# A feature-major first stage in a one-core hybrid diffusion layer: x loaded transposed, norm factors as one row, one visit per step to the row products, two short first steps

## The chip, the cores and the metric

The kernel is one program on one core of a Trainium2 chip. The metric is the device time of one execution in microseconds (us). One execution was also taken by the hardware profiler; all durations below come from that one.

## The reference

One layer with model width D = 2048, 256 latent tokens `x` and 256 context tokens `ctx`. The part that matters here is its beginning: the modulation vectors, the normalised and modulated activations h, and the first of the projections of h.

```python
mod  = (silu(c)     @ w_mod + b_mod)[:, None, :]      # 2048 -> 6 * 2048
modc =  silu(c_ctx) @ w_mod + b_mod
sh1, sc1, g1, sh2, sc2, g2 = split(mod, 6)            # the same for modc
h  = rms_norm(x,   norm_w[0]) * (1 + sc1)  + sh1      # 256 x 2048
hc = rms_norm(ctx, norm_w[0]) * (1 + sc1c) + sh1c
q, ff, fb, v, g, a, b = split(h @ w_in)               # the same for hc; v is 1024 wide
... # recurrence and convolution, output projection, residual, conv FFN, residual
```

`rms_norm(x, w)` is `x * rsqrt(mean(x*x) + 1e-6) * w`. Everything is float32.

## The kernel before

**Number format.** Each float32 operand of a large product is cut into a high part (rounded to fp32r by ScalarE, `self.split`, L976) and a low rest (subtracted by VectorE, L977). One product then takes three matmuls: high by high, high by low, low by high (`mm3_x`, L206 to L208; `mm3_w`, L197 to L199).

**Stages.** The first stage, `phase0`, computes shift and scale for both token sets, h transposed (`hT`: features on the partitions, 16 blocks kb of 128 features, the 512 tokens of x and ctx along the free dimension), and the projection v of all 512 tokens. Then come the gemms of eight heads, with recurrence and convolution work beside them, the output projection, and the FFN up and down.

**The first stage before.** x and ctx arrive token-major in four blocks b of 128 tokens. For each block ScalarE (one of the squares: VectorE) sums the squares (`square_x`), VectorE and GpSimd make the factor (`factor_x`; the power -1/2 is GpSimd's, L229), VectorE scales the block (`scale_x`), and TensorE transposes it, 128 features by 128 tokens at a time (`first_x`, `transpose_x`). The stage runs in eight steps q of two feature blocks:

- `gemv_row(q, t)`, t = 0 to 3: loads 1 MB of `w_mod` and multiplies by silu(c) and silu(c_ctx), four narrow matmuls side by side (L470); after t = 3 ScalarE copies the sums out of PSUM (L475).
- `columns(q)`: four transposes turn these rows into columns (L481), then four small VectorE instructions (L483 to L492) leave scale A and shift B of the step's features.
- `make_h(q)`: ScalarE applies A and B to the transposed x (L510), and `split` writes both parts of `hT`.
- `v0(q, b)` and `v1(q, b)`: the left and right 512 columns of v for token block b. `v0` adds up in PSUM over all steps (`vps`, four banks). `v1` starts a new PSUM tile at each step, which VectorE adds to a running sum in SBUF (`v1_add`, L541). The weights for it (`v_raw`, two SBUF buffers) are split into `vw` by `v_load`.

The row products of step q stand in the program one step ahead of their use, in two visits (t = 0, 1 and t = 2, 3) with `v1` between them. Eight 1 MB buffers (tags raw, whi, wlo in turn) hold the `w_mod` tiles, so loads run two steps ahead. The orders of TensorE and of the DMA queue (SyncE, SP) are written out by hand in the whole stage, those of ScalarE and VectorE only to the end of the hand-written beginning (`self.order(P0_ENG | {ET.Activation, ET.DVE})`); after it a scheduler orders these two by priority. `step(q, b)` runs `transpose_x`, `columns` and `make_h` at high priority. PSUM of the stage: four banks for `vps`, one for the rows, three (tag ax) for everything else. `gemv(n)` starts pieces of the later modulation vectors, which are VectorE work (L713), and `wtile(0)` the first weights of the next stage.

Of the kernel before, what the change touches and what calls it, by code (L numbers as in the profile page):

```python
# [8 lines left out]
F32 = mybir.dt.float32  # L9
# [6 lines left out]
P = 128  # L16
D = 2048
# [12 lines left out]
P0_ROW = 1  # L30
P0_PRIO = 300
P0_X, P0_C = 0, 0
# [13 lines left out]
WIDE, NARROW = (0, 0), (16, 16)  # L46
LEVELS = (1, 2, 4, 8, 16, 32, 64)
# [66 lines left out]
class _Kernel:  # L114
# [126 lines left out]
    def run(self):  # L241
# [43 lines left out]
        p0x, px = enter(name="p0x", bufs=4 - P0_ROW, space=PSUM)  # L285
# [63 lines left out]
    def consts(self):  # L349
# [7 lines left out]
        self.mhalf = cst.tile([P, 2], F32, name="mhalf")  # L357
# [53 lines left out]
    def phase0(self, p0, px, srcs):  # L411
        nc, a = self.nc, self.a
        x0, big = self.x0, self.big
        rstd = p0.tile([P, 4], F32, name="rstd0")

        def load_x(b):
            src = a["x"] if b < 2 else a["ctx"]
            rows = src[0, (b % 2) * P:(b % 2 + 1) * P, :]
            nc.sync.dma_start(x0[:, b, :], rows[:, 0:512])
            nc.sync.dma_start(self.big0[:, b, :], rows[:, 512:1024])  # L420
            nc.sync.dma_start(big[:, :, b, :], rows[:, 1024:].rearrange("p (n c) -> p n c", n=2))

        sums = {}

        def square_x(b, i):

            if i == 0:
                sums[b] = self.sm.tile([P, 5], F32, tag="ss5", name="ss5", bufs=4)
            ss = sums[b][:, i:i + 1]
            src = (x0[:, b, :], self.big0[:, b, :], big[:, :, b, :])[i]  # L430
            if i == 0 and b:
                junk = p0.tile([P, 512], mybir.dt.bfloat16, tag="mkv", name="junkv")
                nc.vector.scalar_tensor_tensor(junk, src, 1.0 / D, src, op0=ALU.mult, op1=ALU.mult, accum_out=ss)
            else:
                junk = p0.tile([P, 2, 512], mybir.dt.bfloat16, tag="mk", name="junk")
                nc.scalar.activation(junk if i == 2 else junk[:, 0, :], src, AF.Square, scale=D ** -0.5, accum_out=ss)

        def factor_x(b):
            ss = sums[b]
            nc.vector.tensor_scalar(ss[:, 3:4], ss[:, 0:1], ss[:, 1:2], EPS, op0=ALU.add, op1=ALU.add)  # L440
            nc.vector.tensor_add(ss[:, 4:5], ss[:, 3:4], ss[:, 2:3])
            self.rsqrt(rstd[:, b:b + 1], ss[:, 4:5])

        def scale_x(b, i):
            x = (x0[:, b, :], self.big0[:, b, :], big[:, :, b, :])[i]
            nc.vector.tensor_scalar_mul(x, x, rstd[:, b:b + 1])

        self.nt = 0
        vps = [self.mm_tile("v") for _ in range(4)]
        vw = self.vx.tile([P, 2, 2, 1024], F32R, tag="vx", name="vw")  # L450
        rows = {}

        vt = p0.tile([P, 4, 256], F32, name="vt")

# [3 lines left out]
        for i in range(2):  # L458
            nc.vector.tensor_copy(cz[:, :, i], self.cs[:, i * KB:(i + 1) * KB])

        def gemv_row(q, t):

            if t == 0:
                rows[q] = px.tile([P, 512], F32, tag="row", name="row", bufs=P0_ROW)
            tag, n = (("raw", 3), ("whi", 3), ("wlo", 2), ("raw", 3), ("whi", 3), ("wlo", 2), ("raw", 3), ("whi", 3))[self.nt % 8]
            self.nt += 1
            w = self.stg.tile([P, 2048 if tag == "raw" else WBUF], F32, tag=tag, name="mraw", bufs=n)[:, 0:2048]
            nc.sync.dma_start(w, a["wm1"][q, t])
            for g in range(4):
                nc.tensor.matmul(rows[q][g * 32:(g + 1) * 32, :], cz[:, t * 4 + g, :], w[:, g * 512:(g + 1) * 512],  # L470
                                 start=t == 0, stop=t == 3)
            if t == 3:
                r = p0.tile([P, 512], F32, tag="rows", name="rows")
                with self.tc.high_priority(P0_PRIO):
                    nc.scalar.copy(r, rows[q])  # L475
                rows[q] = r

        def columns(q):
            col = self.ax_tile("col")
            for i in range(4):  # L480
                nc.tensor.transpose(col[:, i * P:(i + 1) * P], rows[q][:, i * P:(i + 1) * P], self.ident)  # L481
            cv = self.sm.tile([P, 2, 2, 2], F32, tag="cv", name="cv", bufs=2)
            nc.vector.reduce_sum(cv, col.rearrange("p (s j g c) -> p s j c g", s=2, j=2, g=4)[:, :, :, 0:2, :],  # L483
                                 axis=mybir.AxisListType.X)
            A = self.ab[:, 1, q * 2:(q + 1) * 2, :]
            B = self.ab[:, 0, q * 2:(q + 1) * 2, :]
            bsh = self.par("bmod", q * 2, 2).unsqueeze(2).to_broadcast([P, 2, 2])
            bsc = self.bsc1[:, q * 2:(q + 1) * 2].unsqueeze(2).to_broadcast([P, 2, 2])
            nw = self.par("nw", q * 2, 2).unsqueeze(2).to_broadcast([P, 2, 2])
            nc.vector.tensor_add(B, cv[:, 0], bsh)  # L490
            nc.vector.tensor_add(A, cv[:, 1], bsc)
            nc.vector.tensor_mul(A, A, nw)  # L492

# [785 lines left out]
```

## Time and profile before

| | us |
|---|---|
| runs shown (three) | 1422.15, 1422.55, 1440.83; median 1422.55 |
| profiled execution: its own time | 1419.87 |
| profiled execution: span | 1418.1 |
| TensorE busy in the span | 1375.5 (97%) |
| VectorE / ScalarE busy | 1073.3 (76%) / 716.6 (51%) |
| data read | 323.58 MB, 231 GB/s over the span |

The lines of the profile name an instruction by its line, its engine, its operation and its output and input tiles. Times in timelines count from the start of the span. Matmuls are pipelined: the shown duration of one overlaps the next, so the distance between starts is what one costs.

### The profile page before, as it was taken

Reading aid. Unit: us, or ns where it says so; the run is one execution under the profiler, and the core shown is the slowest. Engines: PE = TensorE matmul, PEld = TensorE weight load, DVE = VectorE, ACT = ScalarE, POOL = GpSimd, SP = SyncE. Lnnn points to the kernel's source line nnn. Section 1 sums busy time; section 2 is a strip of 40 time slices with the busy share of each in tenths; the row PEclk is TensorE's granted clock in tenths of the full one; section 3 lists DMA queues with packets and bytes.
Section 4 is the critical chain, followed back from the end, with each engine's and each line's share of the span. In section 5 each row is a group of like instructions: output and inputs, shape, how many; then the busy total and the mean of one; then the engine's idle time right before and its main releaser. Section 6 shows DMA issues by size and latency. Waiting matters only on the chain.

```text
span 1418.1 us, 24793 instructions
## 1 busy us (share of the span) xinstructions
PE 1375.5 (97%) x10272; PEld 1224.9 (86%) x10272; DVE 1073.3 (76%) x1577; ACT 716.6 (51%) x1174; POOL 31.2 (2%) x57
## 2 busy tenths in 40 slices
PE   4999999999999999999999999999999999999997
PEld 2566888888888898988999999999999998888886
DVE  4444788999999899777788788778878886767544
ACT  4333456666656665536744444454545443333532
POOL 0000001001000011000000000000000000000000
PEclk9999999999999999999999999999999999999999
DMA  9988676446645565788355555555555558878652
GB/s 374 391 325 330 258 267 218 160 188 238 222 167 207 208 226 189 286 305 302 123 205 180 205 185 203 181 206 189 199 184 203 193 194 340 312 287 306 242 187 106
DMA packets 49153, 329.38 MB, mean 232 GB/s; under 512 B 5392, under 2 KB 5648, under 8 KB 10896
## 3 DMA queue, kind: packets, MB, share of 16 engines
q1 hardware_dynamic: 49040, 327.80, 62.7%
q8 instruction: 80, 1.31, 0.4%
q14 instruction: 33, 0.27, 0.1%
HBM read 323.58 MB, written 4.19 MB: 231 GB/s over the span
## 4 chain that ended last, share of the span: by engine, by line
PE 77%; DVE 11%; ACT 4%; DMA 3%; issue 2%; POOL 2%; SPq 0%; DVEq 0%; POOLq 0%; ACTq 0%
PE val L197 6%; PE val L199 6%; PE val L198 6%; PE dn L206 6%; PE gate L197 6%; PE dn L208 6%; PE gate L199 5%; PE dn L207 5%; PE gate L198 5%; DVE wlo L140 3%; DVE acc L930 3%; PE v L206 2%; PE wo L208 2%; PE wo L206 2%; PE wo L207 2%
## 5 line engine op out<-in xcount | busy, mean ns | idle before, releaser
L137 ACT CAST whi<-raw 128x2048 fp32r<-128x2048 f32 x193 | 368.9, 1912 | 371.3 <-PE val L198 120.1
L140 DVE TENSOR_TENSOR wlo<-raw,whi 128x2048 fp32r<-128x2048 f32 x193 | 441.9, 2289 | 149.4 <-PE dn L207 59.7
L199 PE MATMUL val<-h,wlo 128*128 128x256 f32 x704 | 194.3, 276 | 0.0
L197 PE MATMUL val<-h,whi 128*128 128x256 f32 x704 | 194.3, 276 | 0.0
L198 PE MATMUL val<-h,whi 128*128 128x256 f32 x704 | 194.3, 276 | 0.0
L197 PE MATMUL gate<-h,whi 128*128 128x256 f32 x688 | 189.9, 276 | 0.0
L198 PE MATMUL gate<-h,whi 128*128 128x256 f32 x688 | 189.9, 276 | 0.0
L199 PE MATMUL gate<-h,wlo 128*128 128x256 f32 x688 | 189.9, 276 | 0.0
L1139 DVE SCALAR_TENSOR_TENSOR gacc<-gate,params,gacc 128x189 f32<-128x189 f32 (+2 forms) x352 | 152.4, 433 | 23.3 <-ACT gacc L1133 12.5
L206 PE MATMUL dn<-whi,hid_hi 128*128 128x512 f32 x352 | 137.4, 390 | 0.0
L208 PE MATMUL dn<-whi,hid_lo 128*128 128x512 f32 x352 | 137.0, 389 | 0.0
L207 PE MATMUL dn<-wlo,hid_hi 128*128 128x512 f32 x352 | 136.9, 389 | 0.0
L197 PEld LDWEIGHTS val<-h,whi 128*128 128x128 f32 x704 | 132.2, 188 | 0.0
L198 PEld LDWEIGHTS val<-h,whi 128*128 128x128 f32 x704 | 132.2, 188 | 0.0
L199 PEld LDWEIGHTS val<-h,wlo 128*128 128x128 f32 x704 | 132.1, 188 | 0.0
L199 PEld LDWEIGHTS gate<-h,wlo 128*128 128x128 f32 x688 | 129.2, 188 | 0.0
L197 PEld LDWEIGHTS gate<-h,whi 128*128 128x128 f32 x688 | 129.1, 188 | 0.0
L198 PEld LDWEIGHTS gate<-h,whi 128*128 128x128 f32 x688 | 129.1, 188 | 0.0
L713 DVE SCALAR_TENSOR_TENSOR big<-graw,cs,big 128x1024 f32<-128x1024 f32 x90 | 113.5, 1278 | 14.0 <-DMA graw<-in_wm_dram 13.9
L930 DVE SCALAR_TENSOR_TENSOR acc<-u,params,acc 128x242 f32<-128x242 f32 (+14 forms) x240 | 98.8, 472 | 0.0
L208 PEld LDWEIGHTS dn<-whi,hid_lo 128*128 128x128 f32 x352 | 66.1, 188 | 13.9
L207 PEld LDWEIGHTS dn<-wlo,hid_hi 128*128 128x128 f32 x352 | 66.1, 188 | 13.5
(270 smaller groups left out, 2681.4 us busy)
## 6 DMA issues: line engine op xcount, KB each, us to landing
raw<-in_wup_dram SPq DMA_DIRECT2D x88, 1024.0 KB, 4.8
graw<-in_wm_dram SPq DMA_DIRECT2D x64, 1024.0 KB, 5.0
raw<-in_win_dram SPq DMA_DIRECT2D x48, 1024.0 KB, 5.0
raw<-in_wdn_dram SPq DMA_DIRECT2D x44, 1024.0 KB, 4.9
mraw<-in_wm_dram SPq DMA_DIRECT2D x32, 1024.0 KB, 9.6
raw<-in_wout_dram SPq DMA_DIRECT2D x16, 1024.0 KB, 4.9
vraw<-in_wv_dram SPq DMA_DIRECT2D x16, 512.0 KB, 6.2
x<-in_x_dram SPq DMA_DIRECT2D x2, 1024.0 KB, 7.1
```

What stands on the lines that cost most here:

```text
L137: self.nc.scalar.copy(hi, raw)
L140: self.nc.vector.tensor_sub(lo, raw, hi.bitcast(F32))
L197: nc.tensor.matmul(out, wh, xh, start=start, stop=False)
L198: nc.tensor.matmul(out, wh, xl, start=False, stop=False)
L199: nc.tensor.matmul(out, wl, xh, start=False, stop=stop)
L206: nc.tensor.matmul(out, xh, wh, start=start, stop=False)
L207: nc.tensor.matmul(out, xh, wl, start=False, stop=False)
L208: nc.tensor.matmul(out, xl, wh, start=False, stop=stop)
L713: nc.vector.scalar_tensor_tensor(self.gacc[:, sl], w[:, sl], c, self.gacc[:, sl], op0=ALU.mult, op1=ALU.add)
L930: nc.vector.scalar_tensor_tensor(d, u[:, lo + o:hi + o], self.par("cw", j * CONVW + k), d, op0=ALU.mult, op1=ALU.add)
L1139: nc.vector.scalar_tensor_tensor(o, g[:, r0 + dy:r1 + dy, c0 + dx:c1 + dx], self.par("fcw", j * 9 + (dy + 1) * 3 + dx + 1), o, op0=ALU.mul ...
```

## The change

x and ctx are laid out on the host as `xt`, features on the partitions: four panels of four feature blocks, 128 x 2048 each, one DMA per panel. Each 512-token slice `xs[kb]` is then what `make_h` needs, without a transpose. The sums of squares now run across partitions: ScalarE squares all 16 slices, VectorE adds them up (`sacc`), four matmuls with a column of ones finish the sums, and a matmul of ones by four diagonal blocks spreads the 512 factors as one row R over all partitions. `scale_x(s)` multiplies a step's slices by R on VectorE.

There are nine steps: feature block 0, feature block 1 (with their own `w_mod` layout `wm0`, two 1 MB tiles each), then seven of two blocks. In each step all row products come in one visit, after `v1` of the step before and directly ahead of `columns` and `make_h` of the same step, with one token block of `v0` between. Token blocks 0 and 1 of `v1` now add up in PSUM over all steps (`va`, two banks), blocks 2 and 3 use one ax bank and VectorE as before; rows and `columns` share one bank. Some spare matmuls (`warm`) stand in the beginning. The host code gains `xt` and `wm0` and loses `ctx`.

```diff
+STEPS = [(0, 1), (1, 1)] + [(kb, 2) for kb in range(2, KB, 2)]
+P0_WARM = 6, 6, 2, 6
-        p0x, px = enter(name="p0x", bufs=4 - P0_ROW, space=PSUM)
+        p0x, px = enter(name="p0x", bufs=1, space=PSUM)
...
     def phase0(self, p0, px, srcs):
...
+        panels = (self.x0, self.big0, self.big[:, 0], self.big[:, 1])
+        xs = [panels[kb // 4][:, kb % 4, :] for kb in range(KB)]
+        last = len(STEPS) - 1
...
+        def square(kb):
+            sq = p0.tile([P, 512], F32, tag="ht", name="sq", bufs=2) if kb else sacc
+            act.activation(sq, xs[kb], AF.Square, scale=D ** -0.5)
+            if kb:
+                dve.tensor_add(sacc, sacc, sq)
+        def sums():
+            ps = self.ax_tile("stat")
+            for b in range(4):
+                nc.tensor.matmul(ps[:, b:b + 1], sacc[:, b * P:(b + 1) * P], self.onecol, start=True, stop=True)
+            st = self.sm.tile([P, 4], F32, name="st0")
+            dve.tensor_scalar_add(st, ps[:, 0:4], EPS)
+            rstd = self.sm.tile([P, 4], F32, name="rstd0")
+            self.rsqrt(rstd, st)
+            dg = p0.tile([P, 4, P], F32, tag="ht", name="dg0", bufs=2)
+            for b in range(4):
+                dve.tensor_scalar_mul(dg[:, b, :], self.ident, rstd[:, b:b + 1])
+            return dg
+        def factors(dg):
+            ps = self.ax_tile("rb")
+            nc.tensor.matmul(ps, ones, dg.rearrange("p b t -> p (b t)"), start=True, stop=True)
+            act.copy(R, ps)
+        def scale_x(s):
+            kb, nk = STEPS[s]
+            for k in range(kb, kb + nk):
+                dve.tensor_mul(xs[k], xs[k], R)
+        def row_load(s):
+            kb, nk = STEPS[s]
+            for t in range(2 * nk):
...
+                nc.sync.dma_start(w, a["wm0"][s, t] if nk == 1 else a["wm1"][kb // 2, t])
+                mraw[s, t] = w
+        def row_mm(s, ts):
+            nk = STEPS[s][1]
+            n, m = 256 * nk, 8 // nk
+            for t in ts:
+                if t == 0:
+                    rows[s] = px.tile([P, 512], F32, tag="row", name="row")
+                w = mraw.pop((s, t))
+                for i in range(m):
+                    g = i % 4
+                    nc.tensor.matmul(rows[s][g * 32:(g + 1) * 32, :n], cz[:, t * m + i, :], w[:, i * n:(i + 1) * n],
+                                     start=t == 0 and i < 4, stop=t == 2 * nk - 1 and i >= m - 4)
+                if t == 2 * nk - 1:
+                    r = p0.tile([P, 512], F32, tag="rows", name="rows")
+                    with self.tc.high_priority(P0_PRIO):
+                        act.copy(r[:, :n], rows[s][:, :n])
+                    rows[s] = r
+        def columns(s):
+            kb, nk = STEPS[s]
+            col = px.tile([P, 512], F32, tag="row", name="col")
+            for i in range(2 * nk):
+                nc.tensor.transpose(col[:, i * P:(i + 1) * P], rows[s][:, i * P:(i + 1) * P], self.ident)
... # reduce_sum and three small VectorE instructions as before, on nk blocks
+        def make_h(s):
... # as before, with xs[kb] in place of the transposed tile
+        va = [px.tile([P, 512], F32, tag="va", name="va", bufs=2) for _ in range(2)]
+        vacc = (None, None, self.x0[:, 0, :], sacc)
+        def v1(s):
+            for b in (2, 0, 3, 1):
+                if b < 2:
+                    v_part(1, s, va[b], b, s == 0, s == last)
+                    continue
+                ps = self.ax_tile("v1")
+                v_part(1, s, ps, b, True, True)
+                if s:
+                    dve.tensor_add(vacc[b], ps, vacc[b])
+                else:
+                    dve.tensor_copy(vacc[b], ps)
+        def step(s):
+            with self.tc.high_priority(P0_PRIO):
+                columns(s)
+                make_h(s)
+        def warm(n):
+            self.keep_warm(n, vps[3][:, 0:P], self.ident, self.ident)
+        self.late_consts()
+        for c in range(4):
+            nc.sync.dma_start(panels[c], a["xt"][c].rearrange("p (k t) -> p k t", k=4))
+        self.start_stream(*srcs)
+        self.order(P0_ENG | {ET.Activation, ET.DVE})
+        row_load(0)
+        raw1 = v_raw(1, 0)
+        row_load(1)
+        raw0 = v_raw(0, 0)
+        row_load(2)
+        for kb in range(KB):
+            square(kb)
+        dg = sums()
+        warm(P0_WARM[0])
+        row_mm(0, [0])
+        warm(P0_WARM[1])
+        factors(dg)
+        row_mm(0, [1])
+        warm(P0_WARM[2])
+        scale_x(0)
+        columns(0)
+        act.copy(vw[:, 1, 0, :512], raw1)
+        make_h(0)
+        dve.tensor_sub(vw[:, 1, 1, :512], raw1, vw[:, 1, 0, :512].bitcast(F32))
+        warm(P0_WARM[3])
+        v_split(0, 0, raw0)
+        scale_x(1)
+        for s in range(1, last + 1):
+            v1(s - 1)
+            raw1, raw0 = v_raw(1, s), v_raw(0, s)
+            row_mm(s, range(2 * STEPS[s][1]))
+            if s + 2 <= last:
+                row_load(s + 2)
+            v_split(1, s, raw1)
+            v0(s - 1, 0)
+            step(s)
+            v0(s - 1, 1, 2, 3)
+            v_split(0, s, raw0)
+            if s == 1:
+                self.order(P0_ENG)
+            if s < last:
+                scale_x(s + 1)
+            if s == 2:
+                self.load_masks(p0)
+            if s == last - 1:
+                self.gemv(P0_E[0])
+            if s == last:
+                self.gemv(P0_E[1])
         self.nxt = self.wtile(0)
+        v1(last)
         self.gemv(P0_E[2])
+        v0(last, 0, 1, 2, 3)
```

Here `v_split(n, s, raw)` is `split` into `vw`, as wide as the step has blocks.

More of the change, by code (lines that the diff above doesn't have):

```diff
@@ L458, in phase0 @@
         for i in range(2):
[L459 to L492, printed above, removed]
```

245 lines of the change are left out of this document (47 added, 198 removed).

## The prediction

> **What bounds the kernel now.** I read the page first, then the stretches of the first stage, then its timeline engine by engine.
>
> ```profile
> span 1418.1 us, 24793 instructions
> PE 1375.5 (97%) x10272; PEld 1224.9 (86%) x10272; DVE 1073.3 (76%) x1577; ACT 716.6 (51%) x1174; POOL 31.2 (2%) x57
> PE 77%; DVE 11%; ACT 4%; DMA 3%; issue 2%; POOL 2%; SPq 0%; DVEq 0%; POOLq 0%; ACTq 0%
> ```
>
> TensorE is busy 97% of the span and carries 77% of the chain that ended last. So the change is worth what it moves the moment at which TensorE finishes v. The stretches (us, busy time and instruction count of each engine, granted clock, share of the DMA engines, GB/s):
>
> ```profile
> 0.00:160.00 160.00, 138.75 (x741) 89.25 (x742) 80.74 (x155) 63.94 (x106) 3.76 (x12) 0.98 0.87 339
> 10.00:20.00 10.00, 6.14 (x34) 0.94 (x34) 1.54 (x3) 0.57 (x2) 0.21 (x1) 1.00 1.01 411
> 20.00:30.00 10.00, 4.32 (x14) 2.94 (x15) 6.22 (x18) 7.30 (x16) 0.55 (x1) 0.74 1.05 402
> 30.00:40.00 10.00, 9.72 (x47) 5.71 (x46) 7.47 (x21) 4.89 (x12) 1.54 (x2) 0.92 1.02 418
> 160.00:672.00 512.00, 499.94 (x4126) 442.61 (x4125) 446.03 (x765) 312.07 (x672) 24.87 (x41) 1.00 0.63 230
> ```
>
> Two regimes: to about 40 us the DMA engines are full and TensorE waits at first; afterwards TensorE is full, and it stays so in the next stage (499.94 of 512). The stage's ends:
>
> ```profile
> 24.12 0.50 PE L206 MATMUL v<-vw,hT 128*128 128x512 f32 x1 [3.40 <-ACT hT L976]
> 157.84 0.39 PE L208 MATMUL v<-vw,hT 128*128 128x512 f32 x1
> 158.90 0.50 PE L197 MATMUL ff<-hT,whi 128*128 128x512 f32 x1 [0.68 <-ACT v L686]
> ```
>
> v starts at 24.12 and issues its last matmul at 157.84, so it ends near 158.07; 0.83 later the next stage starts, after a copy that the change keeps. I count to the end of v.
>
> **The steady step.** One whole step of TensorE before, from one xT group to the next:
>
> ```profile
> 75.42 1.03 PE L502 MATMUL xT<-ident,big 128*128 128x128 f32 x8
> 76.65 0.47 PE L206 MATMUL v<-vw,hT 128*128 128x512 f32 x1
> 80.93 1.92 PE L470 MATMUL row<-mraw,cz 128*32 128x512 f32 x16
> 82.78 0.50 PE L206 MATMUL v<-vw,hT 128*128 128x512 f32 x1
> 88.49 1.92 PE L470 MATMUL row<-mraw,cz 128*32 128x512 f32 x16
> 90.34 0.50 PE L206 MATMUL v<-vw,hT 128*128 128x512 f32 x1
> 91.87 1.03 PE L502 MATMUL xT<-ident,big 128*128 128x128 f32 x8
> 130.27 3.64 PE L470 MATMUL row<-mraw,cz 128*32 128x512 f32 x32
> 133.84 0.50 PE L206 MATMUL v<-vw,hT 128*128 128x512 f32 x1
> 44.81 0.60 PE L481 MATMUL col<-ident,rows 128*128 128x128 f32 x4
> 45.16 0.48 PE L206 MATMUL v<-vw,hT 128*128 128x512 f32 x1
> ```
>
> Starts give: transposes of x with the columns 1.23, 18 v matmuls 4.28, rows 1.85, 24 v 5.71, rows 1.85, 6 v 1.53; together 16.45. An undisturbed v matmul costs about 0.2275; each return from rows adds a few tenths. After the change: 24 v of `v1` 5.60 (no rows ahead of them), one visit of four tiles 3.57 (130.27 to 133.84), 6 v 1.53, the columns alone 0.35 (44.81 to 45.16), 18 v 4.19. That is **15.24, or 1.21 less per step**: 0.88 for the transposes, 0.33 for one visit less.
>
> The step's DMA is 4 x 1024 KB + 2 x 512 KB = 5.24 MB, 12.8 us at 410 GB/s (mean of the three stretches). It fits into 15.24. The Trainium skill, "DMA: Bandwidth & Descriptors", section "Where 436 GB/s comes from", says that some 358 GB/s per core bind between HBM and SBUF; the rows of 402 to 418 disagree, and even by the page the steady step (14.6) would fit, while the beginning below would come out some 5 us later.
>
> What the steps add on other engines is beside TensorE: two multiplications by R per step (0.69 each by the 128x512 row below; a scaling instruction before) against two `v1` additions fewer. VectorE is busy 80.74 of the first 160 us and ScalarE 63.94, so it is covered; uncovered, it would be at most the 1.4 per step of the two multiplications.
>
> **The new wait in each step.** The rows used to be finished a step early. Now the chain rows, copy, columns, h lies inside the step, behind 24 v matmuls in all. Its rows before:
>
> ```profile
> 74.03 0.59 ACT L475 COPY rows<-row 128x512 f32<-128x512 f32 x1 [0.84 <-PE row L470]
> 76.93 0.19 DVE L483 TENSOR_REDUCE cv<-col 128x8 f32<-128x32 f32 x1 [2.48 <-PE col L481]
> 77.69 1.48 ACT L510 ACTIVATE ht<-xT,ab 128x256 f32<-128x256 f32 x3 [3.07 <-DVE ab L492]
> 79.05 0.62 ACT L976 CAST hT<-ht 128x512 fp32r<-128x512 f32 x1
> 80.82 0.69 DVE L977 TENSOR_TENSOR hT<-ht,hT 128x512 fp32r<-128x512 f32 x1 [0.43 <-ACT hT L976]
> ```
>
> The row copy ends 0.75 after the rows; 1.53 of v cover it, 0.78 spare. From the columns' end (76.65) the first high part of h is ready at +3.02 (79.67); `v1` asks for it at +4.19. The last low part is ready at +4.86 (81.51), and the sixth matmul of `v1` asks for it at 4.19 + 5 x 0.2275 = +5.33. So **the least slack is 0.47 us**, and I take the wait at nothing. Behind a late h on ScalarE and VectorE stand the next weights' split and the `v1` additions, and TensorE waits for these too. The other end: one split of weights ahead in both queues:
>
> ```profile
> L977 DVE TENSOR_TENSOR vw<-vraw,vw 128x1024 fp32r<-128x1024 f32 x15 | 18.4, 1226 | 18.3 <-ACT vw L976 18.3
> L976 ACT CAST vw<-vraw 128x1024 fp32r<-128x1024 f32 x15 | 15.7, 1048 | 30.9 <-PE v L208 30.9
> ```
>
> 1.05 + 1.23 - 0.47 = 1.8 us in each of seven steps. The program's places speak for the low end: the right half's split becomes possible when `v1` ends, 3.57 before the chain begins, the left half's when the 18 matmuls end. The single ax bank is the same kind of risk: an addition of 0.69 has the 1.37 of one token block, 0.6 spare.
>
> **The beginning.** Here the DMA order decides. Parameters land at 4.19:
>
> ```profile
> 4.19 0.23 ACT L392 ACTIVATE cs<-params 128x32 f32<-128x32 f32 x1 [2.17 <-DMA params<-in_params_dram]
> vraw<-in_wv_dram SPq DMA_DIRECT2D x1, 512.0 KB, 17.3
> ```
>
> The second row is one 512 KB load issued at 27.66 us: 17.3 us to landing, although it alone takes 1.3. A load waits for all that was issued ahead on SP. After the change the weights of feature block 1 (right half) stand behind the identity 64 KB, x 4096, rows of step 0 2048, a v weight 256, rows of step 1 2048, a v weight 256 and rows of step 2 4096; with their own 256 that is 13120 KB = 13.43 MB, 32.8 us at 410 GB/s: **landing at 37.0** (36.3 to 37.6 by 418 and 402).
>
> The path up to the first v is earlier, by an estimate: x is complete at 14.6; four squares and additions of the last panel 3.4, so 18.0; sums, GpSimd's power, four diagonals, the spreading matmul with spare matmuls and row tiles between; then copy, columns and h, some 3.1. Prices:
>
> ```profile
> 672.69 1.95 PE L87 MATMUL x2T<-dg,x 128*128 128x128 f32 x16
> 674.39 0.48 PE L206 MATMUL wo<-wroom,y_hi 128*128 128x512 f32 x1
> 671.19 0.29 DVE L1113 TENSOR_SCALAR dg<-ident,rs 128x128 f32<-128x128 f32 x1 [0.67 <-POOL rs L229]
> L229 POOL TENSOR_TENSOR rstd<-ss,mhalf 128x1 f32<-128x1 f32 x4 | 2.6, 662 | 30.9 <-DVE ss L441 30.9
> 10.71 1.93 PE L470 MATMUL row<-mraw,cz 128*32 128x512 f32 x8 [10.71 <-DMA mraw<-in_wm_dram]
> ```
>
> A plain float32 matmul of 128 columns costs 0.21 (1.70 for eight), perhaps twice that early, as the row tile of 10.71 took 1.93 against 0.9 later; the 512-wide spreading matmul is not in the trace, and lies between 0.21 and some 1.7 (four times 0.42), with 0.85 taken. With both ends the first v falls between 29 and 33; I take 30, **6 us later than before**. It then does `v1(0)` 2.85, rows of step 1 2.1, left half and columns 3.2: done near 38.
>
> There it stalls. `v_split(1, 1)` stands ahead of `columns(1)` and `make_h(1)` in the hand-written order of both engines: 37.0 + 0.62 + 0.69 + 0.7 + 1.1 + 0.62 = **`v1(1)` starts at 40.7**. Without the weights h of step 1 would come 2.85 + 2.1 + 1.2 + 3.0 = 9.15 after the first v; so a first v later than 31.6 moves it (1.5 at 33); an earlier one doesn't.
>
> Then 12 v 2.8, rows of step 2 3.7, left half and columns 1.2, h 3.0: 51.4. For a cold TensorE I add 1.0:
>
> ```profile
> 24.00:26.00 2.00, 1.88 (x6) 1.36 (x6) 1.38 (x2) 1.97 (x5) 0.00 (x0) 0.68 1.04 385
> 26.00:28.00 2.00, 0.56 (x2) 0.00 (x0) 1.26 (x5) 1.94 (x5) 0.45 (x1) 0.50 1.07 400
> 25.50 0.63 PE L207 MATMUL v<-vw,hT 128*128 128x512 f32 x1
> 25.93 0.63 PE L208 MATMUL v<-vw,hT 128*128 128x512 f32 x1
> ```
>
> After the wait of 3.40 us the granted clock fell to 0.50 and a v matmul cost 0.43; twelve such cost at most 2.4 extra, at least nothing. The Trainium skill, "TensorE: Matmul & The Clock Gate", Part 1, has the clock halve after an idle window of about 3.4 us and recover after as much busy time. The trace agrees (3.40, then 0.50); by that rule the wait of 2.5 us here could fall on either side, which is why I stand between.
>
> So `v1(2)` starts at 52.4. Its weights: behind the other 256 KB and rows of step 3 (4096 KB), 37.0 + 0.6 + 10.2 + 1.3 = 49.1, split by 51.4: just covered. After this the loads run ahead.
>
> **Sum.** 52.4 + 6 x 15.24 = 143.8; the last `v1` and `v0` 48 x 0.2275 + 0.1 = 11.0: end of v at **154.8 against 158.07, 3.2 less**. The profiled execution took 1419.87 around its span of 1418.1, so it would become 1416.7; the median of the runs shown stands 2.7 above it (1422.55), so **1419.4**. The saving of 1.21 in six steps and at the edges is largely spent on the later beginning.
>
> **The rivals.**
>
> - The early loads don't bind (forecast's opposite in the beginning): loads land sooner or the order of the queues hides it. For it: DMA engines reach 418. Against: the 17.3 us row. Without waiting, and with a first v at 29 and no cold clock, `v1(2)` starts at 29 + 9.15 + 2.8 + 3.7 + 4.2 = 48.9, 3.5 earlier: 1416.
> - The chain inside the step takes the place of the transposes: a split or addition of 1.23 gets ahead of h. With 1.0 to 1.8 per step in seven steps, 7 to 12.6 lost, I take 8.4: 1419.4 + 8.4 = 1428. It makes the kernel slower than before from 0.46 per step on (3.2 / 7). For it: the least slack is 0.47, and after step 1 nobody wrote out the order of these two engines. Against: they are half idle, and the step has high priority.
> - The gain is lost behind the stage: the next stage takes the same time to the same waits on loads or VectorE, or its order changes a little: 1422.5. For it: VectorE is busy 446 of 512 there. Against: TensorE 499.94.
>
> **How the numbers follow.** Forecast 0.48 (its own range 1416 to 1422, from the cold clock, 402 to 418 GB/s and 33 for the first v), early loads 0.15, chain 0.20, lost behind 0.17. 1413 to 1428 holds all but the far half of the chain; below 1416 it allows the next stage's order to give as much as it could take (3.1). 2% is 28 us, about what a measurement of this kernel can tell from no change, and no case reaches it (1394 or 1451): the whole stage has at most some 17 us to give (24.1 + 87.4 of v + 25.0 of rows + 2.5 of columns + some 2 of changes between them = 141). So within 2% 0.96; slower 0.03, faster 0.01.
>
> **What would show it.** No xT rows; v from about 30; TensorE waiting for h of step 1 near 38 to 41 and the weights of that step landing near 37; steps 15.2 apart; end of v near 155. Steps of 16 or more with TensorE waiting for hT or for the additions mean the chain. Wrong would be all of it if a wait of the new order that I take as covered sits in each step.

## The result, and the profile after

| | us |
|---|---|
| before, six executions | 1421.93 to 1440.83, median 1422.72 |
| after, six executions | 1466.51 to 1469.52, median 1467.71 |
| ratio after / before | 1.0296, interval 1.0246 to 1.0346 |
| span of the profiled execution | before 1418.1, after 1466.2 |

The kernel is 3% slower, not the same. Some executions of the kernel before and of some experiments are some 20 us longer than the others of the same program (in the profile of e6, which is such a one, it all lies in the FFN up), and one of e8's two ran at a granted clock of 0.852, so the experiments are compared by the parts of their profiles.

The page of the kernel after, its span and the busy time of the engines:

```profile
span 1466.2 us, 24782 instructions
PE 1413.7 (96%) x10290; PEld 1261.9 (86%) x10290; DVE 1074.9 (73%) x1569; ACT 716.6 (49%) x1170; POOL 29.8 (2%) x55
```

TensorE has 38.2 us more busy time, although the change takes the transposes of x from it and adds some spare matmuls. So part of the loss is not waiting but a slower pace, and the first question is in which stage. I cut both spans at the first matmul of the next stage (ff), of the FFN up (gate) and of the FFN down (dn). The stretches of the kernel before (us, busy time and instructions of PE, PEld, DVE, ACT, POOL, clock, DMA share, GB/s):

```profile
158.90:699.40 540.50, 526.82 (x4320) 467.46 (x4321) 467.24 (x803) 333.06 (x716) 26.34 (x43) 1.00 0.61 224
699.40:1167.30 467.90, 467.90 (x4131) 467.90 (x4131) 375.13 (x517) 228.23 (x259) 0.00 (x0) 1.00 0.55 194
1167.30:1418.10 250.80, 243.17 (x1090) 201.25 (x1088) 151.29 (x106) 92.52 (x96) 1.10 (x2) 0.99 0.68 253
```

The same stretches after:

```profile
178.70:719.80 541.10, 532.47 (x4320) 472.98 (x4321) 464.52 (x801) 332.73 (x716) 26.73 (x44) 1.00 0.60 222
719.80:1215.20 495.40, 495.40 (x4131) 495.40 (x4130) 375.01 (x517) 227.82 (x259) 0.00 (x0) 1.00 0.52 183
1215.20:1466.20 251.00, 243.23 (x1090) 201.26 (x1088) 151.06 (x105) 92.50 (x96) 1.08 (x2) 0.99 0.69 253
```

The difference of 48.1 is **19.8 in the first stage** (158.90 to 178.70), 0.6 in the heads, **27.5 in the FFN up** and 0.2 behind it. The FFN up has the same 4131 matmuls, the same full clock and no idle time in both kernels, and the change touches no line of it. Its largest group, before and then after (busy us, mean ns of one):

```profile
L197 PE MATMUL gate<-h,whi 128*128 128x256 f32 x688 | 189.9, 276 | 0.0
```

```profile
L198 PE MATMUL gate<-h,whi 128*128 128x256 f32 x688 | 194.7, 283 | 0.0
```

Every matmul of 256 columns there takes 283 ns in place of 276; by the stretches one comes each 0.1199 us in place of 0.1133 (495.40 / 4131 and 467.90 / 4131).

The first stage after, on TensorE, at the ends of v:

```profile
37.32 0.50 PE L207 MATMUL v<-vw,hT 128*128 128x512 f32 x1 [2.17 <-ACT hT L906]
177.62 0.39 PE L209 MATMUL v<-vw,hT 128*128 128x512 f32 x1
178.73 0.50 PE L198 MATMUL ff<-hT,whi 128*128 128x512 f32 x1 [0.72 <-ACT v L616]
```

v starts 13.2 us later than before (24.12), and ends near 177.85 against 158.07. One step in its middle:

```profile
104.71 3.64 PE L483 MATMUL row<-mraw,cz 128*32 128x512 f32 x32
109.79 0.60 PE L495 MATMUL col<-ident,rows 128*128 128x128 f32 x4
110.15 0.48 PE L207 MATMUL v<-vw,hT 128*128 128x512 f32 x1
114.71 0.49 PE L207 MATMUL v<-vw,hT 128*128 128x512 f32 x1
115.97 0.50 PE L208 MATMUL v<-vw,hT 128*128 128x512 f32 x1 [0.77 <-DVE vw L907]
121.53 3.64 PE L483 MATMUL row<-mraw,cz 128*32 128x512 f32 x32
```

From rows to rows it takes 16.82, not 15.24. The loss sits behind the columns: `v1` waits for the split of the weights. From TensorE's list of waits up to the end of the stage, the two for the weights (total, times, longest):

```profile
PE v L208 <- DVE vw L907: 3.1, 4, 0.8
PE v L207 <- ACT vw L906: 2.2, 1, 2.2
```

And the reason, in the timelines of ScalarE and of VectorE in that step:

```profile
113.12 0.60 ACT L511 ACTIVATE ht<-big,ab 128x256 f32<-128x256 f32 x1
113.63 1.03 ACT L906 CAST vw<-vraw 128x1024 fp32r<-128x1024 f32 x1
114.56 0.62 ACT L906 CAST hT<-ht 128x512 fp32r<-128x512 f32 x1
```

```profile
114.69 1.23 DVE L907 TENSOR_TENSOR vw<-vraw,vw 128x1024 fp32r<-128x1024 f32 x1 [0.75 <-ACT vw L906]
```

The planner (the scheduler that orders these two engines) puts the cast of the weights (113.63) between the two blocks of h. The weights' low part is then ready at 115.92, 1.2 us after TensorE reached `v1`. The raw weights had been there long before: their load went out at 99.11 and the loads of this stretch took 4.6 to 5.8 us, so they lay ready by 104.9, while ScalarE stood idle for 9.12 us up to the row copy at 108.41.

### The profile page after: what moved, and what is told of

Its sections match the earlier page's. It is cut to its first block, busy times and chain, and to the rows that moved or that the text cites. A ratio compares the mean times of both kernels' runs of the same rounds, so it can differ in the third digit from the quotient of the medians.

```text
span 1466.2 us, 24782 instructions
## 1 busy us (share of the span) xinstructions
PE 1413.7 (96%) x10290; PEld 1261.9 (86%) x10290; DVE 1074.9 (73%) x1569; ACT 716.6 (49%) x1170; POOL 29.8 (2%) x55
## 3 DMA queue, kind: packets, MB, share of 16 engines
HBM read 323.58 MB, written 4.19 MB: 224 GB/s over the span
## 4 chain that ended last, share of the span: by engine, by line
PE 76%; DVE 12%; ACT 5%; DMA 3%; issue 2%; POOL 1%; DVEq 0%; SPq 0%; POOLq 0%; ACTq 0%
PE val L199 6%; PE val L198 6%; PE val L200 6%; PE gate L200 6%; PE gate L199 6%; PE gate L198 6%; PE dn L209 5%; PE dn L207 5%; PE dn L208 5%; DVE wlo L141 3%; DVE acc L860 3%; PE wo L207 2%; PE wo L209 2%; PE wo L208 2%; PE row L483 2%
## 5 line engine op out<-in xcount | busy, mean ns | idle before, releaser
L198 PE MATMUL val<-h,whi 128*128 128x256 f32 x704 | 199.2, 283 | 0.0
L199 PE MATMUL val<-h,whi 128*128 128x256 f32 x704 | 199.2, 283 | 0.0
L200 PE MATMUL val<-h,wlo 128*128 128x256 f32 x704 | 199.2, 283 | 0.0
L198 PE MATMUL gate<-h,whi 128*128 128x256 f32 x688 | 194.7, 283 | 0.0
L199 PE MATMUL gate<-h,whi 128*128 128x256 f32 x688 | 194.7, 283 | 0.0
L200 PE MATMUL gate<-h,wlo 128*128 128x256 f32 x688 | 194.7, 283 | 0.0
L198 PEld LDWEIGHTS val<-h,whi 128*128 128x128 f32 x704 | 135.2, 192 | 0.0
L199 PEld LDWEIGHTS val<-h,whi 128*128 128x128 f32 x704 | 135.2, 192 | 0.0
L200 PEld LDWEIGHTS val<-h,wlo 128*128 128x128 f32 x704 | 135.2, 192 | 0.0
L198 PEld LDWEIGHTS gate<-h,whi 128*128 128x128 f32 x688 | 132.1, 192 | 0.0
L199 PEld LDWEIGHTS gate<-h,whi 128*128 128x128 f32 x688 | 132.1, 192 | 0.0
```

Source lines behind the costliest of these rows:

```text
L198: nc.tensor.matmul(out, wh, xh, start=start, stop=False)
L199: nc.tensor.matmul(out, wh, xl, start=False, stop=False)
L200: nc.tensor.matmul(out, wl, xh, start=False, stop=stop)
```

## The experiments

**Theory.** Two independent causes. (1) Place: the change frees 64 bytes in the pool of constants (four `ss5` tiles of 32 bytes each gone, `st0` and `rstd0` of 32 each added), so in the layout of the compiled kernels every tile behind it lies 64 bytes lower (the FFN's weight tile at 47264 in place of 47328), while the FFN's h, laid out from the other end, stays at 196576; the matmuls' pace depends on how the two lie. (2) Order: on the front and in each step ScalarE and VectorE work in an order that TensorE then waits for. **Rivals:** for (1) something of the data flow of the changed first stage (clock, DMA load) slows the FFN; for (2) the loads, or the additions into one bank, pace the steps.

**e1: the 64 bytes put back.** In the kernel after:

```diff
-st = self.sm.tile([P, 4], F32, name="st0")
+st = self.sm.tile([P, 20], F32, name="st0")[:, 0:4]
```

> The changed kernel with 64 bytes more in the pool of constants, so that every tile behind it (the weight tiles whi and wlo among them) starts where it did before the change. Theory 'place': the FFN matmuls of 256 columns became slower (0.1138 to 0.1199 us from start to start, gate to down 467.9 to 495.4 us) only because their weights moved by 64 bytes; expected gate to down back near 468, v matmuls back to 0.2275, time 1467.7 - 27.5 - 2.3 = 1438. Rival 'load': something that the changed first stage does (clock, traffic, another order) slows the FFN; expected no change, 1468.

Measured: median 1438.61, 1.0154 of the kernel before (1.0044 to 1.0264). The FFN up's stretch:

```profile
716.10:1183.90 467.80, 467.80 (x4130) 467.80 (x4129) 375.01 (x517) 228.10 (x259) 0.00 (x0) 1.00 0.55 194
```

467.8 again, as before. One tile's unused bytes give back all 27.5 us; the first stage stays long (ff at 177.4). e1 is the base of all later runs of the changed kernel.

**e3: the kernel before, 64 bytes lower.** The other direction, without any part of the change:

```diff
-sm = cst.tile([P, n], F32, name="lbsm")
+sm = mx
```

> The kernel before with one 64-byte constant tile less, so that all that follows lies 64 bytes lower, as in the changed kernel; no instruction differs otherwise. Theory 'place': gate to down 467.9 to about 495, v matmuls 0.2275 to 0.2335, time 1422.7 + 27.5 + 2.3 = 1452. Rival 'load': 1422.7.

Measured: 1452.73 (two executions). The group of gate in its profile:

```profile
L197 PE MATMUL gate<-h,whi 128*128 128x256 f32 x688 | 194.7, 283 | 0.0
```

283 in a kernel that is otherwise the one before: the place alone does it.

**e4: only the relation.** In the kernel before, weights 128 bytes lower, and the FFN's h moved so that the two stand to each other as in e3:

```diff
-sm = cst.tile([P, n], F32, name="lbsm")
+sm = mx
-cum = cst.tile([P, n], F32, name="lbcum")
+cum = mx
-self.h2 = h2.tile([P, KB, 2, SEQ], F32R, name="h2")
+h2t = h2.tile([P, KB * 2 * SEQ + 32], F32R, name="h2")
+self.h2 = h2t[:, 16:16 + KB * 2 * SEQ].rearrange("p (k i t) -> p k i t", k=KB, i=2)
```

> The kernel before with the weights 128 bytes lower (same place modulo 128) and only h of the FFN (the moving operand) 64 bytes lower modulo 128. If the place of the weights decides by itself: gate to down stays 468, time 1422.7. If the two operands' places against each other decide: both are now at 32 modulo 128, as both were at 96 in the changed kernel, and gate to down becomes about 495, time 1450.

Measured: 1453.57 (two executions), gate again 283 ns. Against e3 both operands start 64 bytes lower: the same difference, the same pace. In e2 below the weights start at the same address as here (47264 in the compiled layout) and h lies 64 bytes higher, and gate takes 279. So it is not the place of one operand alone, but how the two lie to each other.

**e2: the offsets exchanged.** The kernel places wide and narrow weights 16 floats apart inside their tiles:

```diff
-WIDE, NARROW = (0, 0), (16, 16)
+WIDE, NARROW = (16, 16), (0, 0)
```

> The changed kernel with the two start offsets inside the weight buffers exchanged (WIDE and NARROW: 16 and 0 elements, 64 and 0 bytes), nothing else moved. Theory 'place': the FFN weights alone return to their old place modulo 128 bytes; gate to down near 468, the first stage unchanged, time near 1440. If another shifted tile (hidden activations, residual) were the cause: no change, 1468.

Measured: 1462.7. Its groups of gate and dn:

```profile
L198 PE MATMUL gate<-h,whi 128*128 128x256 f32 x688 | 192.0, 279 | 0.0
L207 PE MATMUL dn<-whi,hid_hi 128*128 128x512 f32 x352 | 139.1, 395 | 0.0
```

A miss: 279, half-way, and dn went from 390 to 395. The FFN up takes 486.2 us here, and as much in the profile of e6, whose operands lie where those of e1 do (467.8). With two executions it stays open whether 279 is the pace of these places or what e6 shows.

**e8: 32 bytes put back.**

```diff
-st = self.sm.tile([P, 4], F32, name="st0")
+st = self.sm.tile([P, 12], F32, name="st0")[:, 0:4]
```

> The changed kernel with 32 bytes put back instead of 64, so that all tiles behind the constants lie 32 bytes below their place in the kernel before. Theory 'place, fine': the pace of a matmul depends on the difference of the two operands' places in steps of 32 bytes, so the FFN matmuls of 256 columns come between 276 and 283 ns, the median between 1438 and 1467. Theory 'place, in steps of 64': 283 ns as without any bytes or 276 ns as with 64, the median at one of the two ends.

Measured, in one execution: 1464.0, between the two ends but 3.7 from the one and 25 from the other. In this one execution half of the distance gave a small part of the gain.

**e5: the written order kept.** The program states an order for ScalarE and VectorE and gives it up after step 1. On e1:

```diff
-            if s == 1:
+            if s == last - 2:
                 self.order(P0_ENG)
```

> The changed kernel with the 64 bytes put back and the written order of ScalarE's and VectorE's instructions kept through all steps but the last three, instead of given up after step 1. Theory 'the planner's order': the steps cost 16.7 us because the cast and the subtraction that split the raw weights stand between the blocks of h, and TensorE then waits for both; with the written order the steady step comes to 15.3 us and the steps from 3 on save 4 x 1.4 = 5.6 us, the median about 1431 to 1434. Theory 'DMA': the weights land too late for a shorter step, and the time stays at 1438.6. The first stage's front is untouched in both: first v at 36.

A miss on the bad side: 1442.82 for the profiled execution (1463.67 for the other), and a step of 17.5. The waits for `vw` are gone (3.0 and 2.9 in e1), and another came in TensorE's list of waits:

```profile
PE v L207 <- DVE x L549: 7.6, 7, 1.7
```

The stated order is worse than the planner's, for two reasons that the timelines of ScalarE, VectorE and TensorE show:

```profile
92.95 0.59 ACT L488 COPY rows<-row 128x512 f32<-128x512 f32 x1 [9.78 <-PE row L483]
93.44 1.05 ACT L906 CAST vw<-vraw 128x1024 fp32r<-128x1024 f32 x1
```

```profile
94.52 1.23 DVE L907 TENSOR_TENSOR vw<-vraw,vw 128x1024 fp32r<-128x1024 f32 x1 [5.84 <-ACT vw L906]
95.66 0.18 DVE L497 TENSOR_REDUCE cv<-col 128x8 f32<-128x32 f32 x1
101.87 1.29 DVE L458 TENSOR_TENSOR big<-big,R 128x512 f32<-128x512 f32 x2
103.08 0.69 DVE L549 TENSOR_TENSOR x<-v,x 128x512 f32<-128x512 f32 x1
```

```profile
103.82 0.50 PE L207 MATMUL v<-vw,hT 128*128 128x512 f32 x1 [1.39 <-DVE x L549]
```

The columns' sums (95.66) queue behind a split that queues behind the row copy; and the addition that frees the one ax bank (103.08) queues behind a split and two multiplications, so the next token block waits 1.39.

**e9: an order made for the waits.** On e1, the written order is kept as in e5, but it is another one: the right half's weights are loaded ahead of the step and split ahead of the row products, the left half's split and the multiplication stand behind the additions of `v1`. The masks are loaded later. The main lines:

```diff
         for s in range(1, last + 1):
+            raw1 = v_raw(1, s)
             v1(s - 1)
-            raw1, raw0 = v_raw(1, s), v_raw(0, s)
+            if s > 1:
+                v_split(0, s - 1, raw0)
+            raw0 = v_raw(0, s)
+            scale_x(s)
+            v_split(1, s, raw1)
             row_mm(s, range(2 * STEPS[s][1]))
...
-            if s == 1:
+            if s == last - 2:
                 self.order(P0_ENG)
```

> The changed kernel with the 64 bytes put back, and its steps written out for ScalarE and VectorE in another order up to the last three: the right half's weights are loaded ahead of the step and split as soon as the first products have freed their tile, ahead of the row products; the left half's split and the multiplication by R stand behind the first products' additions. Theory 'order': nothing on TensorE waits in a steady step, and it comes to the 15.24 us of the prediction's sum (against 16.7 with 64 bytes put back alone and 17.5 with the order written as the program states it), so the next stage starts near 168 and not at 177.4. Theory 'something else paces the steps' (the loads, the single bank): the step stays above 16 us. The front is untouched: first v at 36.

Measured: median 1430.25. Row products in TensorE's timeline, and the ff matmuls with their first and last start:

```profile
66.59 3.64 PE L483 MATMUL row<-mraw,cz 128*32 128x512 f32 x32
81.79 3.64 PE L483 MATMUL row<-mraw,cz 128*32 128x512 f32 x32
```

```profile
L198 PE MATMUL ff<-hT,whi x128: 389/389/501, 167.8 to 501.5; 128*128 128x512 f32 x128
```

**The step is 15.20**, without a wait, and the stage is 9.6 us shorter than in e1 (167.8 against 177.4). Order was the steps' cause: neither the loads nor the single bank pace them once it is mended. The edit also sends one load out earlier, but late loads were not what the steps of the kernel after waited for (ready by 104.9, cast at 113.63).

**e6: another front.** On e1: both row tiles and the columns ahead of the sums' spreading, one run of spare matmuls left out (the expectation counts two), three buffers for the squares:

```diff
-            sq = p0.tile([P, 512], F32, tag="ht", name="sq", bufs=2) if kb else sacc
+            sq = p0.tile([P, 512], F32, tag="ht", name="sq", bufs=3) if kb else sacc
...
+        row_mm(0, [0, 1])
         dg = sums()
+        columns(0)
         warm(P0_WARM[0])
-        row_mm(0, [0])
-        warm(P0_WARM[1])
         factors(dg)
-        row_mm(0, [1])
...
-        columns(0)
```

> The changed kernel with the 64 bytes put back, row product and column diagonals put ahead of the spreading of the sums, two runs of spare matmuls dropped, and three buffers for the squares in place of two. Theory 'front': the chain to the first v product is what the two buffers, the spare matmuls and the order of TensorE make it; the sums start near 20, R is there near 26, first v near 30, and the median falls by about 6 us, to 1432.6. Rival 'loads': the second step waits for weights that land at 46 anyway, first v comes early but v of step 1 stays near 48, and the median falls by less than 2 us, to 1437.

Measured: median 1435.71; first v at 33.10, but `v1` of step 1 at 46.91 against 48.09 in e1, and ff only 1.2 earlier (176.2). The size is the rival's, not its reason: ScalarE cast the weights of step 1 at 41.87 without a wait for their load. The timelines of ScalarE and VectorE:

```profile
16.82 0.63 ACT L433 ACTIVATE sq<-big 128x512 f32<-128x512 f32 x1 [0.17 <-DVE sacc L435]
17.62 0.63 ACT L433 ACTIVATE sq<-big 128x512 f32<-128x512 f32 x1 [0.17 <-DVE sacc L435]
```

```profile
39.04 4.90 DVE L458 TENSOR_TENSOR big<-big,R 128x512 f32<-128x512 f32 x8
```

With three buffers the squares still come every 0.80 us and wait for `sacc`: the buffers did not pace the loop, the chain of additions did. And eight multiplications for later steps (39.04 to 43.94) stand ahead of the split and the columns of step 1, so the early first v is lost again. In this profile the matmuls of the FFN up take 281 ns, and the FFN up 486.2 us against 467.8 in e1.

**e7: e5 and e6 together.**

> Both edits together on the changed kernel with the 64 bytes put back. If the two causes add, the median is about 1421 to 1426, even with the kernel before (1420.8 beside the run with the 64 bytes); if the loads take back what the front gains, about 1431; if the order does nothing either, 1437.

Measured: median 1441.28 (1437.22 to 1455.18). A miss: it has the steps of e5 (17.5), and the front's gain does not reach past them (ff at 180.4 against 180.6 in e5).

**e10: a third front.** On e1, with two accumulators in turn, the matmuls that finish the sums between the two row tiles, and the first split ahead of R; also three buffers for the squares and two runs of spare matmuls less. The main lines:

```diff
+            acc = (sacc, R)[kb % 2]
-                dve.tensor_add(sacc, sacc, sq)
+                dve.tensor_add(acc, acc, sq)
...
+        row_mm(0, [0])
         dg = sums()
+        row_mm(0, [1])
+        columns(0)
+        v_split(1, 0, raw1)
         factors(dg)
```

> The changed kernel with the 64 bytes put back and a front in which two accumulators take the squares in turn, so that no addition waits for the one just before it, the column sums stand between the two row tiles, and the first weights are split before R is there. Theory 'chain of additions': with three buffers for the squares the loop still took 0.795 us per slice, so the chain of additions paced it, and the loop now takes some 0.63 per slice, the sums start near 20.5 and the first v near 30 (33.1 with the other front). Theory 'the loads of x pace it': sums stay at 22.4 and first v near 32. The steps behind it stay as the planner orders them, at 16.7 us.

Measured: median 1433.2, first v at 30.37. The additions in VectorE's timeline, and the last four squares in ScalarE's:

```profile
15.55 0.69 DVE L436 TENSOR_TENSOR R<-R,sq 128x512 f32<-128x512 f32 x1
16.15 0.69 DVE L436 TENSOR_TENSOR sacc<-sacc,sq 128x512 f32<-128x512 f32 x1
19.94 0.69 DVE L439 TENSOR_TENSOR sacc<-sacc,R 128x512 f32<-128x512 f32 x1
```

```profile
16.75 2.19 ACT L434 ACTIVATE sq<-big 128x512 f32<-128x512 f32 x4 [0.28 <-DMA big<-in_xt_dram]
```

0.60 apart where nothing else holds them (0.64 per slice over the whole loop), and the sums are ready near 20.6. Both as expected. What is left of the loop is the load: the last squares wait for x until 16.75.

**e11: e9 and e10 together, and e12: with the tail.** e12 keeps the written order through the last step but one (masks and two `gemv` tiles behind it), and in steps 1 and 2 puts the right half's split behind the columns. e12 against e11:

```diff
+            if s > 2:
-            v_split(1, s, raw1)
+                v_split(1, s, raw1)
...
                 columns(s)
+                if s < 3:
+                    v_split(1, s, raw1)
                 make_h(s)
...
-            if s == last - 2:
+            if s == last - 1:
                 self.order(P0_ENG)
```

> Both edits on the changed kernel with the 64 bytes put back. If both causes are right, the first stage ends some 18 us earlier than with the 64 bytes alone (some 9 by the steps, 8 at the front, where the weights of step 1 land near 37 and v of step 1 starts near 40): the next stage starts near 160, as in the kernel before (158.9), and the time is within 0.3% of the kernel before's. If the loads of the beginning take the front's gain, the next stage starts near 166.

> As the run before it, with two more edits: the written order holds through the last step but one (masks and the first two tiles of the products of the later modulation follow after it), and in steps 1 and 2, whose weights land late, the right half's split stands behind the columns and not ahead of the row copy. In the run before, the step that the planner ordered took 18.9 us (row products at 124.00 and 142.91) where the others took 15.2, and the row copies of steps 1 and 2 held up TensorE for 2.2 and 0.9. Theory: these 3.7 + 2.2 + 0.9 come off, the next stage starts near 158 and the median is near 1418, equal to or up to 3 us below the kernel before's fast executions (1418 to 1422). Rival: the last steps wait for their loads, or the products moved behind them cost the last step what they had cost the others; the next stage starts near 162 to 165 and nothing is won.

Measured: e11 median 1424.44 (1422.42 to 1425.55), ff at 164.8, near its second figure (166): the row copy of step 1 stood behind a cast that waited for the late weights. e12 median 1420.05 (1417.31 to 1425.69), 0.9976 of the kernel before (0.9943 to 1.0009). TensorE's timeline of e12, and its ff matmuls:

```profile
31.44 0.50 PE L207 MATMUL v<-vw,hT 128*128 128x512 f32 x1 [1.38 <-ACT hT L908]
42.21 0.50 PE L207 MATMUL v<-vw,hT 128*128 128x512 f32 x1 [2.05 <-ACT hT L908]
54.57 0.50 PE L207 MATMUL v<-vw,hT 128*128 128x512 f32 x1 [1.68 <-ACT hT L908]
77.64 3.64 PE L485 MATMUL row<-mraw,cz 128*32 128x512 f32 x32
92.84 3.64 PE L485 MATMUL row<-mraw,cz 128*32 128x512 f32 x32
```

```profile
L198 PE MATMUL ff<-hT,whi x128: 387/389/502, 160.3 to 492.4; 128*128 128x512 f32 x128
```

ff starts at 160.3, between the theory's 158 and the rival's 162, and 1.4 later than before. The steady steps are 15.2, but the one behind the third line still takes 17.5 (`v1` of the next step starts at 72.09): TensorE waits once more for h (0.25 before 56.21), and five matmuls then come 0.42 apart (granted clock 0.50 from 56.5 to 58.5). With place and order mended the change wins nothing that can be measured: its cheaper steps pay for its later beginning, and no more.

## Why the prediction was wrong

Predicted 1419.4 with 0.96 on no change; measured 1467.7. Of the profiled spans (1414.9 would have been the prediction's, 1466.2 came), 27.5 lie in the FFN up, 23.0 in the first stage (v ending at 177.85, not 154.8), the rest of 0.8 between and behind. Of the 23.0, 10.3 had been lost when `v1(2)` started (62.67, not 52.4), 10.8 came in the six steps behind it (17.04 in the mean, not 15.24), and 2.0 in the last products (12.97, not 11.0).

- **The FFN, 27.5: a step that the sum did not have.** The sum took everything behind the stage as unchanged. The rival "the gain is lost behind the stage" looked at the next stage's waits, and bounded what lies behind by TensorE's idle time. That a removed tile of constants moves all others was in the diff; that the place sets the pace of 4131 matmuls no row of before could show, but WIDE and NARROW, two offsets of 64 bytes, stood in the code unexplained. e1, e3 and e4 show it.
- **The new wait in each step, "I take the wait at nothing": the step that failed in the stage.** The slack of 0.47 follows from the rows of before, and the place of the danger was named ("one split of weights ahead in both queues"), but the wrong end was taken: the split became possible early, and the planner issued it late all the same. Measured 16.82 for the step in place of 15.24, of which 0.1 is place (16.72 in e1). The rival "chain" priced this 1.0 to 1.8 per step and had 0.20.
- **The steady step, 15.24: right as TensorE's own work**, 15.20 in e9 and in e12. So were its parts up to the columns (in the step above 5.08 for the rows with six v, 5.10 in the sum; 0.36 for the columns, 0.35).
- **First v at 30: wrong by 7.3.** "Four squares and additions of the last panel 3.4, so 18.0" let the loads pace the squares. One chain of 15 additions paced them, 0.80 from start to start ((11.83 - 0.69) / 14), by VectorE's timeline of the kernel after:

```profile
10.46 11.83 DVE L435 TENSOR_TENSOR sacc<-sacc,sq 128x512 f32<-128x512 f32 x15 [3.27 <-ACT sq L433]
```

  It ended at 22.3, 4.3 late. Spare matmuls and a row tile then held the spreading matmul until 30.85 (its diagonals were ready at 26.6), and seven multiplications by R for later steps, which "it is covered" had priced at nothing, went into the first chain, four of them ahead of the first low part of h. TensorE and VectorE there:

```profile
30.85 1.02 PE L452 MATMUL rb<-dg,ones 128*128 128x512 f32 x2
```

```profile
35.35 2.49 DVE L458 TENSOR_TENSOR big<-big,R 128x512 f32<-128x512 f32 x4
```

  e10 takes these away and starts at 30.37. That it meets the 30 is partly luck: "x is complete at 14.6" was early by 2.1 (16.75 in e10), the sums came at 20.6 and not at 18.0, and the path behind them took 9.7 where the forecast had 12. The 2.1 is a matter of the loads: "a load waits for all that was issued ahead on SP" is not all. In e11 the weights of step 1 land at 39.22, 2.2 late as well, and by then its DMA engines had moved some 14.7 MB, 0.8 more than what was issued up to that load with the parameters (13.9): an estimate from the GB/s of its stretches, worth 2.0 us at 410.
- **Weights of feature block 1 at 37.0, `v1(1)` at 40.7: wrong.** The queue was not full to that point, as I had it. SP stood for 17.0 us before a `vraw` buffer that was not free until the first split was done. Two stretches of the kernel after, SP's timeline, and TensorE's inside `v1(0)`:

```profile
10.00:20.00 10.00, 0.00 (x0) 0.00 (x0) 8.30 (x12) 7.94 (x14) 0.00 (x0) 1.00 1.01 425
36.00:41.00 5.00, 2.11 (x7) 1.15 (x7) 5.00 (x10) 1.75 (x4) 0.00 (x0) 0.93 0.25 89
```

```profile
39.12 0.88 SPq L524 DMA_DIRECT2D vraw<-in_wv_dram  x2
```

```profile
39.09 0.50 PE L208 MATMUL v<-vw,hT 128*128 128x512 f32 x1 [1.27 <-DVE vw L584]
```

  89 GB/s between 36 and 41; the two loads went out from 39.12 on and had landed by 44.7 (3.1 to 5.0 us each). Late as they were, they did not set `v1(1)`, which started at 49.75: ScalarE cast its weights at 46.03, straight behind the row copy and without a wait for a load. By the forecast's own terms it was the first v, 5.7 later than the 31.6 that they could bear, and `v1(0)`, which took 6.44 (37.32 to 43.76) in place of 2.85: TensorE waited for the first weights' low part, and matmuls then came 0.43 apart. 40.7 + 5.7 + 3.6 gives 50.0. In e12, which makes the first split before R is there and so frees the buffer early, `v1(1)` starts at 42.21 and `v1(2)` at 54.57, 1.5 and 2.2 from the predicted times, and there the loads do decide: ScalarE waits for them until 39.89 and 51.83. The Trainium skill, "DMA: Bandwidth & Descriptors", section "Where 436 GB/s comes from", with its 358 GB/s per core, would by an estimate have put these weights at 41.7 (13.43 MB behind 4.19). The 425 of the first row disagrees, and where the buffer is free early they land at 39.22 (e11) and 39.89 (e12).
- **The 1.0 for a cold TensorE: it came, but elsewhere.** The forecast puts it behind the wait ahead of `v1(1)`. In the kernel after, matmuls of v come 0.43 apart, not 0.23, from 41.49 to 43.20 and from 64.33 to 67.32 (granted clock 0.55 from 41 to 44, 0.53 from 64 to 67), behind waits of 2.17 and 1.27, and of 2.22 and 0.77. In e12 a wait of 2.05 ahead of `v1(1)` has no such matmuls behind it, and waits of 1.68 and 0.25 have five. So the length of one wait does not tell, and none of these is as long as the 3.40 of before.

The number 1419.4 nearly came out in e12 (1420.05). That is luck and does not make the forecast right: it priced an order of work that the changed program did not have, and in e12 too v ends near 159.5, not at 154.8, so that nothing of the 3.2 that it gave the stage is there.

## What to carry to other kernels

When a diff adds or removes even a small tile, compare the start addresses of all matmul operands in the two layouts before reading anything else, and if a stage that the diff does not touch changes its nanoseconds per matmul, put the bytes back first. A slack is worth nothing where a planner orders the queue: list what else is ready for that queue in that window, and price it as if it went first. Before a load is priced by what was issued ahead of it, look for the buffer that it needs and who frees it. A sum over slices into one accumulator takes the full time of each addition and more; two in turn overlap.

## What the runs showed of the hardware

- The pace of matmuls depends on the start addresses of weights and moving operand to each other. In the FFN up (256 columns), with the start of the weights minus that of h modulo 256 bytes, from the compiled layouts: 64 gives 276 ns (the kernel before, e1), 0 gives 283 (e3, e4 and the kernel after), and 192 gave 279 in e2; one matmul each 0.1133 against 0.1199 us. A difference of 0 is not bad everywhere: dn (512 columns, with the hidden activations as the stationary operand) has it in all other runs, and in e2, the only one with another (192), its largest group went from 390 to 395. The Trainium skill, "TensorE: Matmul & The Clock Gate", section "Step-by-step: what each phase is for", has two independent read ports, so that loading the next weights takes no read bandwidth from the running matmul. By that alone the places of the two operands to each other should not matter; in e3 and e4, which differ from the kernel before only in places, they do (283 against 276). Why it is so, and whether the period is 256 bytes, stays open: 32 bytes were tried once.
- The addresses are not all: the placement that gave 276 ns in e1's profile ran at 281 through the whole FFN up in e6's (486.2 us against 467.8), at granted clocks of 0.995 and 0.994. What sets this is open.
- Additions of 128x512 on VectorE that each need the last one's sum come every 0.80 us (the kernel after, and e6 with a third buffer), two sums in turn every 0.60, though each addition shows 0.69 (e10).
